# Value projection from the raw split of x, value weights ahead of token-major x, and an opening ordered by hand

## The chip, the cores and the metric

The kernel runs on one core of a Trainium2 chip. The metric is the device time of one execution in microseconds (us). "Before" is the kernel without the change, "after" the kernel with it. Both are written on top of a planner: the program states operations and tiles, and the planner assigns buffers, inserts the semaphores and orders the instructions of each engine by priority (program order) and by its own estimate of times, except inside blocks marked as a manual schedule, where the named engines keep the order of the program.

The five engines are TensorE (PE, with the weight loads as PEld), VectorE (DVE), ScalarE (ACT), GpSimd (POOL) and SyncE (SP), which issues nearly all DMAs.

## The reference

A trunk of two layers on one sequence of 512 tokens with 1024 channels, in float32. The change touches only the first step of the first layer, the forgetting attention:

```python
hn = rmsnorm(x, g[0])                      # x * rsqrt(mean(x*x) + 1e-6) * g
proj = hn @ w_in                           # w_in: 1024 x (3*1024 + 16): q, k, v, forget logits
f_logit = proj[..., 3*D:] + b_f            # 16 heads
log_f = log_sigmoid(f_logit)
c = cumsum(log_f, axis=1)
s = (q * 64**-0.5) @ k.T + c[:, None] - c[None, :]    # causal, per head of 64
o = softmax(s) @ v
...
x = x + rmsnorm(o @ w_out, g[1])
```

After it come a squared-ReLU MLP (1024 to 4096 to 1024) and a gated per-layer embedding, then a second layer of the same kind whose mixer is a gated short convolution.

## The kernel before

**Numbers as pairs.** A float32 operand of a matmul is split into a high part (rounded by ACT: a copy into the matmul's type) and a low part (the rest, a subtraction on DVE), and a product is three matmuls: high x high, high x low, low x high (`mm3`, `split`). For weights of the first projection the gain g of the norm is multiplied in while splitting (`split_gained`). x comes a second time from memory already transposed (`xT`, eight tiles of 128x512, `raw_x`), and its norm's factor 1/rms is applied later: to v when it leaves PSUM (`keep_values`), and to the transposed x itself (`normed_x`), which gives `hT`, the normalised and split x with tokens along the free dimension.

**Chunks of v.** v and the forget logits are computed for four blocks t of 128 tokens in three chunks of columns (`V_CHUNKS`): chunk 0 has 272 columns (256 of v and the 16 logits), chunk 1 has 512, chunk 2 has 256. Chunks 0 and 1 use the raw split `turned` (`of_x`) as the stationary operand, chunk 2 uses `hT`. Then `project(i)` makes q and k of heads 2i and 2i+1 from `hT`; `scores`, `turn` and `mix` are the attention itself. The split k (kh and kl) is copied by DMA to the other half of the partitions. `logs` computes log_f, `sums_of_logs` sums it by matmuls with a triangle of ones (`tri`), writes the sums to memory, and `bias(h)` reads them back as rows for head h.

**1/rms.** The mean squares come from x a third time, token-major (`first_x`, tiles xc): one half by ACT, one half by DVE (`mean_squares`), and the power -1/2 by POOL (`inverse`). `rows_of` makes a diagonal of them on POOL and a matmul with ones turns it into rows (bank `r_rows`) for `normed_x`.

**Loads and splits of weights.** `fetch(n)` issues the loads of weight tiles up to the n-th, in the order that `plan` recorded: chunk 0 of v (tiles 0 to 7), chunk 1 (8 to 15), chunk 2 (16 to 19, each two contraction tiles wide), then q and k (from 20 on, four tiles for each pair of heads), and so on. There are 14 buffers for raw weights, so tile n + 14 waits until tile n is split. `prepare(n)` splits up to the n-th.

**Order.** SP's queue begins with chunk 0's weights and xT, then four tiles of xc, then six of chunk 1's weights, then the other four of xc and the bias of the logits. A manual block holds PE, DVE, ACT and POOL in the program's order through chunk 0 up to the point where chunk 0's v is kept:

```python
        banks_v = [bank(f"v0_{t}") for t in range(NB)]
        with tc.manual_schedule(engines={E.PE, E.DVE, E.Activation, E.Pool}):
            ...
            for t in range(NB):
                keep_values(0, t, banks_v[t])
```

Behind that the planner orders: the triangle, the logs, chunk 1 with `rows_of` and `normed_x` between its blocks, the sums of logs, chunk 2, and `project(0)`. There are eight PSUM banks of 128x512 for everything and 70 SBUF pages of 128x512.

Of the kernel before, what the change touches and what calls it, by code (L numbers as in the profile page):

```python
# [8 lines left out]
F32 = mybir.dt.float32  # L9
# [6 lines left out]
P = 128  # L16
D = 1024
S = 512
# [50 lines left out]
def trunk(ctx: ExitStack, tc, x, xT, pT, g, gT, wv, wqk, bf, wo, wci, wcq, cw, wco, wup, wdn, wpp, wpg, out):  # L69
# [13 lines left out]
    def bank(name):  # L83
        return psum.tile([P, S], F32, tag="ps", name=name)
# [189 lines left out]
    def split(hi, lo, src, eng=nc.vector):  # L274

        nc.scalar.copy(hi, src)  # L276
        return eng.tensor_tensor(out=lo, in0=src, in1=hi.bitcast(F32), op=ALU.subtract)  # L277
# [131 lines left out]
                         f"{kind}r")  # L409
                then(t)  # L410

    def attention(hT, raw_x, first_x, b_f, work, by_hand):
        vs = [[None] * 4 for t in range(NB)]
        n_f = NB * H
        logit = stat("logit", n_f)
# [3 lines left out]
        def logs():  # L419

            e, u, lg = stat("f_e", n_f), stat("f_u", n_f), stat("f_l", n_f)
            neg = stat("f_n", n_f)
            nc.vector.tensor_scalar(out=neg, in0=logit, scalar1=-1.0, scalar2=None, op0=ALU.mult)
            nc.vector.tensor_tensor(out=neg, in0=logit, in1=neg, op=ALU.min)
            nc.scalar.activation(e, neg, AF.Exp)
            nc.vector.tensor_scalar(out=u, in0=e, scalar1=1.0, scalar2=None, op0=ALU.add)
# [5 lines left out]
            nc.vector.reciprocal(ru, u)  # L432
            nc.vector.tensor_tensor(out=rest, in0=rest, in1=ru, op=ALU.mult)
            nc.vector.tensor_tensor(out=lg, in0=lg, in1=rest, op=ALU.subtract)
# [4 lines left out]
            split(lf.hi, lf.lo, logf)  # L439

        def sums_of_logs(tri):
            ps_c = bank("ps_c")
# [23 lines left out]
        def of_x(k, t):  # L466
            return turned[t, k // 4].at(lambda h: h[:, k % 4 * P : k % 4 * P + P])

        def part(ps, t, n):

            for p, of in ("hi", "hi"), ("hi", "lo"), ("lo", "hi"):
                for k in range(4 * n, 4 * n + 4):
                    nc.tensor.matmul(
                        ps[:, : V_CHUNKS[0][1]], getattr(of_x(k, t), p),
                        getattr(ready["v", 0, k], of),
                        start=k == 0 and p == of, stop=k == KT - 1 and p == "lo",
                    )

        def values(c, t):

            width = V_CHUNKS[c][1]
            ps = bank(f"v{c}_{t}")
            for k in range(KT):
                if width == 256:
                    w = wide("v", c, k // 2).at(lambda u: u[:, k % 2 * 256 : k % 2 * 256 + 256])
                else:
                    w = wide("v", c, k)
                mm3(ps[:, :width], of_x(k, t) if c == 1 else tokens(hT, k, t), w, k == 0, k == KT - 1)
            keep_values(c, t, ps)

        def keep_values(c, t, ps):

            c0, width = V_CHUNKS[c]
            n_v = min(width, D - c0)
            if n_v < width:
                nc.vector.scalar_tensor_tensor(
                    out=logit[:, t * H : (t + 1) * H], in0=ps[:, n_v:width], scalar=rs[t],
                    in1=b_f, op0=ALU.mult, op1=ALU.add,
                )
            splits = []  # L500
            for c1 in range(0, n_v, 256):
                i = (c0 + c1) // 256
                vs[t][i] = page(f"v{t}_{i}", F32R)
                src = ps[:, c1 : c1 + 256].rearrange("p (i e d) -> p i e d", e=2, d=HD)
# [3 lines left out]
                    lo = block[:, :, 64 + 64 * e : 128 + 64 * e]  # L508
                    splits.append((hi, lo, src[:, :, e, :]))
            for hi, _, src in splits:  # L510
                if c < 2:
                    nc.scalar.mul(hi, src, rs[t])
                else:
                    nc.scalar.copy(hi, src)
            for hi, lo, src in splits:
                if c < 2:
                    nc.vector.scalar_tensor_tensor(
                        out=lo, in0=src, scalar=rs[t], in1=hi.bitcast(F32),
                        op0=ALU.mult, op1=ALU.subtract,
                    )  # L520
                else:
                    nc.vector.tensor_tensor(
                        out=lo, in0=src, in1=hi.bitcast(F32), op=ALU.subtract
                    )

        stacked, probs, outs, both = {}, {}, {}, {}

# [170 lines left out]
        name = "n0"  # L698
        E = mybir.EngineType

        def mean_squares(t):
            half = lambda n: first_x[t][n][:, :S]
            q = squares(half(0), f"{name}_q0_{t}"), products(half(1), f"{name}_q1_{t}")
            v = stat(f"{name}_v{t}")
            nc.vector.tensor_tensor(out=v, in0=q[0], in1=q[1], op=ALU.add)
            return v

        def inverse(t, v):
            r = stat(f"{name}_r{t}")
            nc.gpsimd.tensor_tensor(out=r, in0=v, in1=neg_half, op=ALU.pow)  # L710
            return r

        all_ones = page("all_ones")
        nc.gpsimd.memset(all_ones[:, :P], 1.0)
        r_rows = []

        def rows_of(t):
            if not r_rows:
                r_rows.append(bank("r_rows"))
            d = page(f"r_d{t}")  # L720
            nc.gpsimd.tensor_scalar(
                out=d[:, :P], in0=ident, scalar1=rs[t], scalar2=None, op0=ALU.mult
            )
            nc.tensor.matmul(
                r_rows[0][:, t * P : (t + 1) * P], all_ones[:, :P], d[:, :P],
                start=True, stop=True,
            )

        def normed_x(t):
            for n in range(2):  # L730
                h = raw_x[t][n][:, :S].rearrange("p (j c) -> p j c", j=4)
                r = r_rows[0][:, t * P : (t + 1) * P].unsqueeze(1).to_broadcast([P, 4, P])
                nc.vector.tensor_tensor(out=h, in0=h, in1=r, op=ALU.mult)
                to = lambda u: u[:, 4 * n : 4 * n + 4, t * P : (t + 1) * P]
                split(to(hT.hi), to(hT.lo), h)

        banks_v = [bank(f"v0_{t}") for t in range(NB)]
        with tc.manual_schedule(engines={E.PE, E.DVE, E.Activation, E.Pool}):
            work(9)
            split_x(0, 0)  # L740
            prepare(4)
            part(banks_v[0], 0, 0)
            split_x(0, 1)
            split_x(1, 0)
            part(banks_v[1], 1, 0)
            prepare(KT)
            part(banks_v[0], 0, 1)
            split_x(1, 1)
            part(banks_v[1], 1, 1)
            for t in (2, 3):  # L750
                for n in range(2):
                    split_x(t, n)
                    part(banks_v[t], t, n)
            for t in range(2):
                rs[t] = inverse(t, mean_squares(t))
                prepare(KT + 2 * t + 2)
            prepare(RAWS)
            for t in (2, 3):
                rs[t] = inverse(t, mean_squares(t))
            prepare(2 * KT)  # L760
            for t in range(NB):
                keep_values(0, t, banks_v[t])
        tri = page("tri", F32R)
        ones = page("ones")
        nc.gpsimd.memset(ones[:, :S], 1.0)
        nc.gpsimd.affine_select(
            out=ones[:, :S], in_=ones[:, :S], compare_op=ALU.is_ge, fill=0.0, base=0,
            pattern=[[1, S]], channel_multiplier=-1,
        )
        nc.vector.tensor_copy(tri[:, :S], ones[:, :S])  # L770
# [386 lines left out]
    with tc.manual_schedule(engines={mybir.EngineType.SP, mybir.EngineType.Activation}):  # L1157
# [13 lines left out]
        b_f = consts.tile([P, H], F32, tag="bf", name="b_f")  # L1171
        nc.sync.dma_start(b_f, bf[0:1, :].partition_broadcast(P))
    warm_p = bank("warm_p")

    def work(n):
# [6 lines left out]
    lhs, opened = attention(hT, raw_x, first_x, b_f, work, by_hand)  # L1182
    oT = lhs
    lhs = lambda k, t: tokens(oT, k, t)
    kind = "o"
# [120 lines left out]
```

## Time and profile before

| | us |
|---|---|
| median of 3 runs | 1230.01 |
| lowest and highest of them | 1228.50 and 1230.23 |
| the profiled execution | 1231.56 |
| its span, first to last instruction | 1229.8 |
| mean granted TensorE clock in it | 0.995 |
| PE busy from 0 to 100 us of the span | 91.38 |
| PE busy from 100 to 200 us | 100.00 |
| PE busy from 200 to 300 us | 98.75 |

The profile is of one execution. Times in its views count from the start of the span. A row of the timeline gives start, length, engine, line of the kernel, operation, written and read tiles, shapes, the number of instructions merged into the row, and in brackets how long the engine had been idle before and what ended that. Rows of SPq and ACTq are issues of DMAs. A row of the table of stretches gives the stretch, its length, busy time and number of instructions for each engine, the granted clock, the share of the DMA engines' time and their rate.

### The profile page before, as it was taken

The page shows a single profiled execution, that of the slowest core. Times are in us where ns is not written, and L with a number is a line of the kernel's source. Part 1 is how long each engine was busy: PE and PEld are TensorE (multiplying, and loading weights), DVE is VectorE, ACT ScalarE, POOL GpSimd, SP SyncE. Part 2 cuts the span into 40 slices and gives each one's busy share as a digit, 9 for nine tenths or more (in the row PEclk, how much of TensorE's full clock was granted, in tenths as well). Part 3 has the DMA queues.
Part 4 walks back from the last instruction along what each step waited for, and adds up shares of the span by engine and source line. Part 5 has one row for each costly group of instructions (what it writes and reads, how often), then busy time and mean ns, then how long its engine had stood idle before and what let it go on. Part 6 is the DMA issues. An engine that isn't in the chain of part 4 may idle for free.

```text
span 1229.8 us, 18755 instructions
## 1 busy us (share of the span) xinstructions
PE 1213.2 (99%) x6175; PEld 1030.7 (84%) x6175; DVE 932.0 (76%) x1474; ACT 690.2 (56%) x1465; POOL 657.1 (53%) x617
## 2 busy tenths in 40 slices
PE   8999999999999999999999999999999999999997
PEld 6778888798888888888889999989888888888886
DVE  6958889676787767869777798766876897669873
ACT  6747778656744644465567444445756345635551
POOL 2016566235876787866213255315677777778310
PEclk9899999999999999999999999999999999999999
DMA  9375554442343234328232133542422443245401
GB/s 313 122 184 152 153 170 130 145 164 70 120 138 95 82 99 137 120 65 288 76 104 88 50 102 96 155 159 91 129 75 71 138 137 95 61 120 164 179 8 61
DMA packets 87314, 150.84 MB, mean 123 GB/s; under 512 B 10352, under 2 KB 18080, under 8 KB 87216
## 3 DMA queue, kind: packets, MB, share of 16 engines
q1 hardware_dynamic: 86640, 149.11, 39.3%
q8 instruction: 49, 0.80, 0.3%
q10 hardware_dynamic: 576, 0.53, 0.1%
q14 instruction: 49, 0.40, 0.1%
HBM read 139.03 MB, written 6.37 MB: 118 GB/s over the span
## 4 chain that ended last, share of the span: by engine, by line
PE 88%; DMA 4%; issue 2%; DVE 2%; ACT 2%; POOL 2%; SPq 0%; POOLq 0%; DVEq 0%; ACTq 0%
PE up L268 9%; PE up L269 9%; PE up L270 9%; PE dn L268 8%; PE dn L269 8%; PE dn L270 8%; PE qk L270 2%; PE qk L269 2%; PE pg L268 2%; PE qk L268 2%; PE pg L270 2%; PE pg L269 2%; PE pT L597 1%; PE co L268 1%; PE co L269 1%
## 5 line engine op out<-in xcount | busy, mean ns | idle before, releaser
L277 DVE TENSOR_TENSOR wl<-raw,wh 128x512 fp32r<-128x512 f32 x346 | 347.5, 1049 | 14.2 <-ACT wh L276 13.4
L269 PE MATMUL up<-hTh,wl 128*128 128x512 f32 (+1 forms) x576 | 210.2, 365 | 0.0
L270 PE MATMUL up<-hTl,wh 128*128 128x512 f32 (+1 forms) x576 | 209.6, 365 | 0.0
L268 PE MATMUL up<-hTh,wh 128*128 128x512 f32 (+1 forms) x576 | 208.7, 366 | 0.0
L276 ACT CAST wh<-raw 128x512 fp32r<-128x512 f32 x346 | 189.4, 625 | 4.5 <-DVE xd L373 4.4
L958 ACT ACTIVATE r<-up 128x512 f32<-128x512 f32 (+1 forms) x72 | 39.4, 548 | 202.1 <-PE up L270 188.3
L277 POOL TENSOR_TENSOR wl<-dn_T,wh 128x512 fp32r<-128x512 f32 x96 | 132.7, 1414 | 30.1 <-ACT wh L276 30.1
L268 PEld LDWEIGHTS up<-hTh,wh 128*128 128x128 f32 x576 | 108.6, 189 | 17.6
L269 PEld LDWEIGHTS up<-hTh,wl 128*128 128x128 f32 x576 | 108.6, 189 | 17.4
L270 PEld LDWEIGHTS up<-hTl,wh 128*128 128x128 f32 x576 | 108.3, 189 | 17.6
L168 POOL TENSOR_TENSOR dn_T<-raw,raw 128x512 f32<-128x512 f32 x56 | 85.8, 1544 | 69.4 <-DMA raw<-in_wdn 58.1
L1004 DVE TENSOR_TENSOR acc<-dn,acc 128x512 f32<-128x512 f32 x168 | 107.4, 680 | 13.9 <-PE dn L270 13.8
L168 POOL TENSOR_TENSOR dn_T<-raw,dn_T 128x512 f32<-128x512 f32 x56 | 93.3, 1666 | 2.2
L276 ACT CAST wh<-dn_T 128x512 fp32r<-128x512 f32 x112 | 61.4, 616 | 11.0 <-POOL dn_T L168 11.0
L277 DVE TENSOR_TENSOR A12l<-q,A12h 128x512 fp32r<-128x512 f32 x28 | 22.3, 798 | 53.8 <-ACT A12h L276 53.8
L1018 POOL TENSOR_TENSOR acc<-acc,acc 128x512 f32<-128x512 f32 x28 | 46.9, 1709 | 9.9 <-DVE acc L1004 9.9
L270 PE MATMUL qk<-hTl,wh 128*128 128x512 f32 x128 | 51.1, 400 | 0.0
L269 PE MATMUL qk<-hTh,wl 128*128 128x512 f32 x128 | 51.1, 399 | 0.0
L268 PE MATMUL qk<-hTh,wh 128*128 128x512 f32 x128 | 50.7, 396 | 0.0
L269 PE MATMUL pg<-wh,hTl 128*128 128x512 f32 x128 | 50.5, 394 | 0.0
L268 PE MATMUL pg<-wh,hTh 128*128 128x512 f32 x128 | 50.4, 394 | 0.0
L277 DVE TENSOR_TENSOR A11l<-q,A11h 128x256 fp32r<-128x256 f32 x28 | 22.6, 807 | 36.5 <-ACT A11h L276 36.5
(413 smaller groups left out, 3328.7 us busy)
## 6 DMA issues: line engine op xcount, KB each, us to landing
raw<-in_wup SPq DMA_DIRECT2D x128, 256.0 KB, 2.9
raw<-in_wdn SPq DMA_DIRECT2D x128, 256.0 KB, 2.8
raw<-in_wcq SPq DMA_DIRECT2D x36, 256.0 KB, 2.8
raw<-in_wqk SPq DMA_DIRECT2D x32, 256.0 KB, 5.3
raw<-in_wpg SPq DMA_DIRECT2D x32, 256.0 KB, 4.4
g<-in_g SPq DMA_DIRECT2D x22, 256.0 KB, 5.7
prl<-neg_c SPq DMA_DIRECT2D x16, 256.0 KB, 6.4
raw<-in_wo SPq DMA_DIRECT2D x16, 256.0 KB, 3.9
```

Source lines behind the costliest of these rows:

```text
L168: ins = nc.gpsimd.tensor_tensor(out=B[name], in0=B[a], in1=B[b], op=op)
L268: nc.tensor.matmul(ps, a.hi, b.hi, start=start, stop=False)
L269: nc.tensor.matmul(ps, a.lo, b.hi, start=False, stop=False)
L270: nc.tensor.matmul(ps, a.hi, b.lo, start=False, stop=stop)
L276: nc.scalar.copy(hi, src)
L277: return eng.tensor_tensor(out=lo, in0=src, in1=hi.bitcast(F32), op=ALU.subtract)
L597: nc.tensor.transpose(ps[:, b * P : (b + 1) * P], probs[h][b][:, j * P : (j + 1) * P], ident)
L958: nc.scalar.activation(r[:, :n], ps[:, :n], AF.Relu)
L1004: ins = nc.vector.tensor_tensor(out=a, in0=banks[s], in1=a, op=ALU.add)
L1018: nc.gpsimd.tensor_tensor(out=a, in0=a, in1=acc[i, s][:, :S], op=ALU.add)
```

## The change

Chunk 2 of v is computed from the raw split too, and its 1/rms is applied when it leaves PSUM as for the other chunks, so `hT` is read only by `project`. The weights of v's second chunk are loaded ahead of all of xc, and those of the third behind it; SP is in the manual block as well. The block now reaches to the end of `normed_x` and to chunk 1's `keep_values`: its order for PE is chunk 0, chunk 1 (now by halves of the contraction, all products with the high weights first), with the matmuls for the rows of 1/rms once, in the middle of block 2. All mean squares are on ACT; `stats` does their end on POOL. The triangle is made at the start of POOL's work. The logs are cut into three steps between which chunk 1's blocks are kept. `normed_x` runs over one half of the channels for all four blocks, then the other. Outside the block stand chunk 2, with the sums of logs and the first two heads' bias after its second block, and `project(0)`.

```diff
-        def values(c, t):
-            width = V_CHUNKS[c][1]
-            ps = bank(f"v{c}_{t}")
+        def values(t):
+            ps = bank(f"v2_{t}")
             for k in range(KT):
...
-                mm3(ps[:, :width], of_x(k, t) if c == 1 else tokens(hT, k, t), w, k == 0, k == KT - 1)
-            keep_values(c, t, ps)
+                w = wide("v", 2, k // 2).at(lambda u: u[:, k % 2 * 256 : k % 2 * 256 + 256])
+                mm3(ps[:, :256], of_x(k, t), w, k == 0, k == KT - 1)
+            keep_values(2, t, ps)
...
-        def rows_of(t):
...
+        def inverse(t):
+            rs[t] = stats(t, first_x[t], name)
             nc.gpsimd.tensor_scalar(
+                out=r_d[:, t * P : (t + 1) * P], in0=ident, scalar1=rs[t], scalar2=None,
+                op0=ALU.mult,
             )
+        def rows():
+            ps = bank("r_rows")
+            for t in range(NB):
+                at = slice(t * P, (t + 1) * P)
+                nc.tensor.matmul(
+                    ps[:, at], warm[:, :P].bitcast(F32), r_d[:, at], start=True, stop=True
+                )
+            return ps
+        def normed_x(n, r_rows):
+            halves = [raw_x[t][n][:, :S].rearrange("p (j c) -> p j c", j=4) for t in range(NB)]
+            def low(t):
+                to = lambda u: u[:, 4 * n : 4 * n + 4, t * P : (t + 1) * P]
+                split(to(hT.hi), to(hT.lo), halves[t])
+            for t, h in enumerate(halves):
+                r = r_rows[:, t * P : (t + 1) * P].unsqueeze(1).to_broadcast([P, 4, P])
                 nc.vector.tensor_tensor(out=h, in0=h, in1=r, op=ALU.mult)
+                if t:
+                    low(t - 1)
+            low(NB - 1)
...
+        with tc.manual_schedule(engines={E.PE, E.DVE, E.Activation, E.Pool, E.SP}):
...
             prepare(KT)
-            part(banks_v[0], 0, 1)
+            fetch(2 * KT)
+            first_x = [load_x("xc", t) for t in range(NB)]
+            nc.sync.dma_start(b_f, bf[0:1, :].partition_broadcast(P))
+            fetch(2 * KT + 4)
+            halves(0, (0, 1))
...
+            nc.vector.tensor_copy(tri[:, :S], ones[:, :S])
+            prepare(KT + 4)
+            halves(1, (0, 0), (1, 0))
             prepare(2 * KT)
+            halves(1, (0, 1), (1, 1))
             for t in range(NB):
-                keep_values(0, t, banks_v[t])
...
-        logs()
+                inverse(t)
+            halves(1, (2, 0))
+            r_rows = rows()
+            halves(1, (2, 1), (3, 0), (3, 1))
+            for two in ((0, 1), (2, 3)):
+                for t in two:
+                    logits(t, banks_v[0, t])
+                for t in two:
+                    keep_values(0, t, banks_v[0, t])
+                prepare(2 * KT + 4)
+            steps = logs()
+            next(steps)
+            keep_values(1, 0, banks_v[1, 0])
+            next(steps)
+            keep_values(1, 1, banks_v[1, 1])
+            next(steps)
+            normed_x(0, r_rows)
+            keep_values(1, 2, banks_v[1, 2])
+            normed_x(1, r_rows)
+            keep_values(1, 3, banks_v[1, 3])
         for t in range(NB):
-            values(1, t)
-            if t in (0, 2):
-                rows_of(t)
-                rows_of(t + 1)
-            if t:
-                normed_x(t - 1)
-        sums_of_logs(tri)
-        normed_x(3)
-        bias(0)
-        bias(1)
-        for t in range(NB):
-            values(2, t)
+            values(t)
+            if t == 1:
+                sums_of_logs(tri)
+                bias(0)
+                bias(1)
         for _ in project(0):
             pass
...
             if t == 1:
                 fetch(KT)
-        first_x = [load_x("xc", t) for t in range(2)]
         fetch(RAWS)
-        first_x += [load_x("xc", t) for t in (2, 3)]
```

More of the change, by code (lines that the diff above doesn't have):

```diff
@@ L699, in attention @@
         E = mybir.EngineType
[L701 to L711, printed above, removed]
@@ L713, in attention @@
-        all_ones = page("all_ones")
-        nc.gpsimd.memset(all_ones[:, :P], 1.0)
-        r_rows = []
-        def rows_of(t):
-            if not r_rows:
-                r_rows.append(bank("r_rows"))
-            d = page(f"r_d{t}")
+        r_d = page("r_d")
+        def inverse(t):
+            rs[t] = stats(t, first_x[t], name)
             nc.gpsimd.tensor_scalar(
-                out=d[:, :P], in0=ident, scalar1=rs[t], scalar2=None, op0=ALU.mult
-            )
[L724 to L727, printed above, removed]
@@ L735, in normed_x, with halves @@
-                split(to(hT.hi), to(hT.lo), h)
-        banks_v = [bank(f"v0_{t}") for t in range(NB)]
-        with tc.manual_schedule(engines={E.PE, E.DVE, E.Activation, E.Pool}):
+                if t:
+                    low(t - 1)
+            low(NB - 1)
+        with tc.manual_schedule(engines={E.PE, E.DVE, E.Activation, E.Pool, E.SP}):
             work(9)
+            banks_v = {(0, t): bank(f"v0_{t}") for t in range(NB)}
+            def halves(c, *at):
+                for t, n in at:
+                    if (c, t) not in banks_v:
+                        banks_v[c, t] = bank(f"v{c}_{t}")
+                    part(c, banks_v[c, t], t, n)
@@ L748, in attention @@
             split_x(1, 1)
-            part(banks_v[1], 1, 1)
+            halves(0, (1, 1))
             for t in (2, 3):
@@ L752, in attention @@
                     split_x(t, n)
[L753 to L759, printed above, removed]
+                    halves(0, (t, n))
+            tri, ones = page("tri", F32R), page("ones")
+            nc.gpsimd.memset(ones[:, :S], 1.0)
+            nc.gpsimd.affine_select(
+                out=ones[:, :S], in_=ones[:, :S], compare_op=ALU.is_ge, fill=0.0, base=0,
+                pattern=[[1, S]], channel_multiplier=-1,
+            )
```

69 lines of the change are left out of this document (23 added, 46 removed).

## The prediction

> **What bounds the kernel now.** I read the page first, then a table of stretches, then the waits and the timelines of the first 90 us, engine by engine. The page's first part says who is the bound:
>
> ```profile
> PE 1213.2 (99%) x6175; PEld 1030.7 (84%) x6175; DVE 932.0 (76%) x1474; ACT 690.2 (56%) x1465; POOL 657.1 (53%) x617
> ```
>
> TensorE has work in all but 16.6 of 1229.8 us, so a change elsewhere counts only where TensorE stands still or runs slow. The change touches the opening alone. The stretches there are v's first chunk, its second chunk, its third chunk with the sums of logs, then q and k of the first heads, then the first scores. Columns: stretch and its length; busy time with instructions of PE, PEld, DVE, ACT, POOL; granted clock; DMA share; GB/s.
>
> ```profile
> 0.00:19.40 19.40, 17.52 (x106) 15.32 (x107) 10.69 (x21) 11.49 (x21) 1.44 (x9) 1.00 0.89 300
> 19.40:45.80 26.40, 24.14 (x105) 18.09 (x104) 22.09 (x62) 19.23 (x51) 6.38 (x9) 1.00 0.84 281
> 45.80:65.40 19.60, 17.39 (x112) 15.80 (x111) 17.21 (x44) 10.70 (x30) 0.29 (x1) 0.83 0.16 20
> 65.40:81.00 15.60, 15.57 (x70) 12.55 (x68) 8.57 (x19) 9.29 (x22) 2.47 (x7) 1.00 0.78 228
> 81.00:87.80 6.80, 4.58 (x15) 3.81 (x16) 3.50 (x12) 3.54 (x7) 0.70 (x2) 0.75 0.63 158
> ```
>
> The third and fifth stretch also lose clock. Busy time overstates TensorE, since the ends are modelled, so I count spacings from its timeline (start, length, engine, line, operation, tiles, shapes, count, idle before).
>
> ```profile
> 19.39 0.40 PE L268 MATMUL v<-wh,xh 128*128 128x512 f32 x1
> ...
> 26.30 0.50 PE L268 MATMUL v<-wh,xh 128*128 128x512 f32 x1 [1.74 <-ACT wh L285]
> ...
> 36.03 0.39 PE L268 MATMUL v<-wh,xh 128*128 128x512 f32 x1
> ...
> 38.08 0.39 PE L268 MATMUL v<-wh,xh 128*128 128x512 f32 x1
> ...
> 45.78 0.40 PE L445 MATMUL ps_c<-tri,lf_h 128*16 128x512 f32 x1
> ...
> 47.17 0.33 PE L268 MATMUL v<-wh,hTh 128*128 128x256 f32 x1
> ...
> 47.93 0.28 PE L268 MATMUL v<-wh,hTh 128*128 128x256 f32 x1
> ...
> 50.09 0.30 PE L268 MATMUL v<-wh,hTh 128*128 128x256 f32 x1
> 51.21 0.38 PE L268 MATMUL v<-wh,hTh 128*128 128x256 f32 x1 [0.81 <-ACT hTh L276]
> ...
> 54.57 0.58 PE L269 MATMUL v<-wh,hTl 128*128 128x256 f32 x1 [0.60 <-DVE hTl L277]
> ...
> 65.37 0.40 PE L270 MATMUL qk<-hTl,wh 128*128 128x512 f32 x1
> ...
> 82.23 0.30 PE L581 MATMUL sc<-kh,qs 128*128 128x128 f32 x1 [1.26 <-DMA kh<-kh]
> 83.52 0.33 PE L582 MATMUL sc<-kl,qs 128*128 128x128 f32 x1 [1.00 <-DMA kl<-kl]
> ```
>
> Nine matmuls of 512 columns lie between 36.03 and 38.08: 0.228 us each. Eighteen of 256 columns lie between 47.93 and 50.09: 0.120 each. The second chunk has 4 blocks x 8 tiles x 3 products = 96 matmuls of 512 columns, 21.9 us; it took 45.78 - 19.39 = 26.4. The matmuls for the rows of 1/rms in it are worth some 0.7, so 3.8 us are lost, 1.74 of them at one stop for a late weight. From 47.17 to 65.37 the third chunk took 18.2 us for 96 matmuls of 256 columns (11.5) and four qk ones set between them (0.9): 5.8 lost, about 3 in stops for the normalised x (hT) and the rest at a halved clock. **Together 9.6 us** between 19.4 and 65.4 are no work. A third loss comes at the first scores: 1.26 + 1.00 of idle and, at clock 0.75, 0.25 x 6.8 = 1.7 of slow matmuls, together 4.0.
>
> **The change part by part.**
>
> *Loads.* v's second-chunk weights move ahead of the token-major x. On the queue of SP and on ACT and DVE the order was:
>
> ```profile
> 8.76 2.14 SPq L381 DMA_DIRECT2D xc<-in_x  x4
> ...
> 16.85 2.81 SPq L381 DMA_DIRECT2D xc<-in_x  x4
> ...
> 14.18 1.28 ACT L276 CAST xh<-xT 128x512 fp32r<-128x512 f32 x2 [1.84 <-DMA xT<-in_xT]
> ...
> 18.19 1.37 ACT L285 ACTIVATE wh<-raw,first_g 128x512 fp32r<-128x512 f32 x2 [1.97 <-DMA raw<-in_wv]
> ...
> 19.46 0.62 ACT L312 ACTIVATE junk<-xc 128x512 f32<-128x512 f32 x1
> 19.98 0.18 ACT L312 ACTIVATION_READ_ACCUMULATOR junk<-xc 128x1 f32 x1
> ...
> 25.53 1.38 ACT L285 ACTIVATE wh<-raw,first_g 128x512 fp32r<-128x512 f32 x2 [1.32 <-DMA raw<-in_wv]
> ...
> 18.95 1.42 DVE L287 SCALAR_TENSOR_TENSOR wl<-raw,first_g,wh 128x512 fp32r<-128x512 f32 x2 [1.79 <-ACT wh L285]
> ```
>
> Five transfers of 256 KB (four of xc and the first weight) lie between xT's last landing at about 14.5 and 18.15: 0.735 each. Without the four, weights 8 to 15 land from 15.2 to 20.4, the eight of xc by 26.3, b_f at 26.4, the third chunk's four weights by 29.3. On SP weights 14 and 15 wait for the buffers of weights 0 and 1, whose splits stand ahead of nearly all of x: no stop. ACT is free of x at 15.5 and splits a weight in 0.65 to 0.69, DVE in 0.7: weights 8 to 11 are done at about 19.3, with TensorE at 19.39; 12 to 15 at about 22.1, needed at 19.39 + 24 x 0.228 = 24.9. The 3.8 us go. What is late next is xc: ACT's eight squares (0.62 and a read of 0.18, overlapping by some 0.1) follow the landings, from 22.5 for block 0 to 27.0 for block 3. POOL then has three steps a block, two on 128x1 and the diagonal, of which the last is:
>
> ```profile
> 27.50 2.81 POOL L721 TENSOR_SCALAR r_d<-ident,n_r 128x128 f32<-128x128 f32 x4
> ```
>
> At 0.7 for each of the twelve they end by 22.5 + 8.4 = 30.9. The rows' matmuls come at 24.9 + 5.5 + 2.7 = 33.1, so TensorE's own work hides them with 2 us to spare. With four banks for chunk one, three for chunk two and one for the rows, block 3 of chunk two needs a bank that `keep_values(0, 0)` frees; DVE can start on that when b_f is in at 26.5 and ends at about 28.1, while TensorE wants it at 33.1 + 0.6 + 2.7 = 36.4. Nothing is lost there, and it would take 8 us more to lose anything. Moving the tri mask to the start of POOL's queue costs DVE a copy of 0.4 behind which weight 8 waits; that is within the cover above to some 0.1 us. So the second chunk ends at 19.39 + 21.9 + 0.6 = 41.9 instead of 45.8.
>
> *Third chunk from the raw split.* It no longer reads hT, so it follows at once: 11.5 us, and the sums of logs 1.4 (45.78 to 47.17). TensorE reaches q and k at 54.8. The 5.8 us go, and the price is that DVE must have hT and the first wqk tile by then. In DVE's queue, by these rows:
>
> ```profile
> 34.32 0.55 DVE L432 RECIPROCAL f_ru<-f_u 128x64 f32<-128x64 f32 x1
> ...
> 42.50 1.13 DVE L517 SCALAR_TENSOR_TENSOR v<-v,n_r,v 128x128 fp32r<-128x128 f32 x4 [0.32 <-ACT v L512]
> ...
> 48.63 3.67 DVE L733 TENSOR_TENSOR xT<-xT,r_rows 128x512 f32<-128x512 f32 x6
> ...
> 53.25 0.67 DVE L450 COPY c_T<-ps_c 16x512 f32<-16x512 f32 x1
> 53.85 3.68 DVE L277 TENSOR_TENSOR hTl<-xT,hTh 128x512 fp32r<-128x512 f32 x6
> ...
> 58.64 3.24 DVE L287 SCALAR_TENSOR_TENSOR wl<-raw,first_g,wh 128x256 fp32r<-128x256 f32 x8
> ```
>
> from 26.5 on stand, in the order written: chunk one kept (8 x 0.28 and four logits, 3.1), four weight tiles (8 x 0.41 = 3.3), the logs (nine steps on 128x64, of which this is the longest: under 5, I take 2.1), chunk two kept (16 x 0.28 = 4.5), hT (8 x 0.61 twice, 9.8). That is 22.8 us of work. It waits besides for ACT's halves, for the third chunk's weights until 29.3, for ACT's table load ahead of Ln, and for block 3 of chunk two at 41.9; following these steps in order I get hT whole at about 53 and the list's end at 54.8. Tile by tile q and k want hT's second half only at 54.8 + 12 x 0.228 = 57.5: covered by 4. The first wqk tile, behind the list, is split at 55.6: TensorE waits 0.8 for it. Bounds: 0, if the planner sets that tile into one of DVE's waits, and 1.3 of wait with clock loss behind it. I take 0.6, near the walk. Later tiles cost DVE 0.82 and TensorE 1.37, so it doesn't fall behind again.
>
> What a wait costs in clock is where row and rule differ. At 54 to 56 us the clock is down after stops of 0.8 at most:
>
> ```profile
> 54.00:56.00 2.00, 1.43 (x6) 0.50 0.00 0
> ```
>
> By the 1.7 us of slow matmuls behind the scores' stops, 1.3 of wait could cost 3.0. The Trainium skill ("TensorE: Matmul & The Clock Gate", Part 1: The HAM clock gate) has the clock halve after an idle window of about 3.4 us; by that the wait of 0.8 costs itself alone and the sum stays what it is. The trace disagrees in part: no single stop here was that long, several short ones in a row were enough.
>
> *Rest of the diff.* Squares on ACT instead of half on DVE, and the scale by 1/rms in keeping chunk three (16 instructions, each no dearer than chunk two's 0.28): below 1 us on engines with cover. DVE's four products and sums of them that go free nothing that anyone waits for.
>
> *First scores.* They come 72 qk matmuls behind 54.8, at 71.2; now it is 65.37 + 68 x 0.228 = 80.9. They wait for kh and kl copied across partitions:
>
> ```profile
> 65.96 7.90 SPq L158 DMA_DIRECT2D raw<-in_wqk  x7
> 74.52 0.53 SPq L553 DMA_DIRECT2D kh<-kh  x1
> ...
> 71.25 0.68 DVE L277 TENSOR_TENSOR kl<-qk,kh 64x512 fp32r<-64x512 f32 x1 [1.48 <-ACT kh L276]
> ```
>
> kl was ready at 71.9, its copy queued behind seven weights on SP. k of the first heads ends on TensorE as far ahead of the scores as before, SP still refills the weight buffers in between, and DVE is busier (about 8 wqk tiles at 0.82 and chunk three behind the list). So the loss of 4.0 can go (copies issued at once) or grow by some 3 to 6 (DVE's backlog). I take it as unchanged.
>
> **Sum:** 9.6 - 0.6 = 9.0 us off. The profiled run took 1231.56 (span 1229.8 and 1.76 around it), so 1222.6; it lies 1.55 above the median of the runs, 1230.01, so for the median **1221.0**. Its own range: 13.6 off if the scores' stop goes too (1216.4), 6 off if the wait costs 3.0 and clock (1224).
>
> **The rivals.** *DVE becomes the bound.* It was busy 17.2 of 19.6 us in the third stretch; the same work, less 8 us of time. For it: the walk ends 0.8 late already. Against: 65.4 to 81.0 shows 8.6 of 15.6 busy, room to catch up. If kl is made 4 to 6 us later against TensorE than before, the gain is 9.0 less that: 3 to 5 off, 1225 to 1227.
>
> *The bias of the logs comes too late (slower).* From the start of c_T (53.25) to the last mask of head 0 took 16.3 us:
>
> ```profile
> 69.01 0.49 POOL L569 TENSOR_SCALAR_AFFINE_SELECT prl<-prl 128x128 f32<-128x128 f32 x1 [0.73 <-DMA prl<-neg_c]
> ```
>
> That used to be ready 12.7 us before the first scores (82.2). Now TensorE is 9.6 earlier, and c_T stands on DVE behind the list and perhaps behind eight wqk tiles: 54.8 + 6.6 = 61.4, ready at 77.7. Without bias DVE can't empty the scores' banks; TensorE goes on through six banks of about 1.7 us (six qk matmuls and two scores), to 81.4. From c_T at 65.1 on each us costs one; at 74.1 the gain is gone, at 79 it is 5 slower: 1235. Against it: 13 us of delay on DVE that I see no work for.
>
> *The loads don't bring it.* If the weights landed no earlier, 3.8 of the 9.6 stay: 5.2 off, 1224.8. Against: the spacing of 0.735 leaves room on each tile. I count it with the first rival.
>
> **How the numbers follow.** About 0.2% (2.5 us) is what a measurement of this kernel can tell from no change. Forecast 0.63; DVE as the bound or late loads, still over 2.5 faster, 0.19; most of the gain lost, within 2.5, 0.05; the late bias or another loss of that sign in the newly ordered rest 0.13. The range goes from 1217.0 (13 off) to 1228.0, which takes in the forecast's range and the first rival and leaves the last two cases out.
>
> **What would show it.** Right: no stop of TensorE above 0.5 us from 19.4 to 54, the last v matmul near 54 and the 72nd qk one near 71, clock 1.00 in 50 to 60, ACT's first 512-wide weight near 16, xc issued behind all of wv1. Wrong: a stop for hT or wl of over 2 us at the first qk matmul, scores waiting beyond 77, a mask on neg_c as the releaser of DVE's score steps, or a part behind 100 us that became longer.

## The result: the opening came forward as predicted, the time did not

| | before | after |
|---|---|---|
| median, us | 1229.96 | 1231.87 |
| lowest and highest | 1227.55 and 1232.10 | 1229.94 and 1233.45 |
| runs | 13 | 13 |
| span of the profiled execution | 1229.8 | 1230.4 |
| mean granted clock in it | 0.995 | 0.994 |

The ratio of after to before is 1.0018, with an interval of 1.0009 to 1.0026: slower by 0.1 to 0.3%. The forecast was 1221.0, its range 1217.0 to 1228.0. The result lies outside.

The table of stretches of after, cut at the points that answer to those of before (columns as there):

```profile
0.00:20.42 20.42, 18.74 (x105) 16.96 (x106) 14.65 (x26) 15.57 (x27) 1.81 (x9) 1.00 0.93 306
20.42:43.12 22.70, 22.70 (x106) 18.91 (x105) 13.04 (x43) 15.89 (x46) 6.31 (x12) 1.00 0.74 263
43.12:55.84 12.72, 12.72 (x105) 12.22 (x104) 11.76 (x26) 9.02 (x23) 0.00 (x0) 1.00 0.01 3
55.84:72.35 16.51, 16.51 (x74) 13.34 (x72) 13.87 (x36) 12.52 (x33) 0.88 (x3) 1.00 0.59 173
72.35:83.38 11.03, 0.00 (x0) 0.03 (x1) 0.00 (x0) 1.01 (x1) 1.47 (x5) 0.64 0.75 192
83.38:90.20 6.82, 6.16 (x19) 5.07 (x20) 5.03 (x17) 3.78 (x11) 1.55 (x2) 0.58 0.40 108
```

Rows two to four are the change at work: from 20.42 to 72.35 TensorE has no gap and the full clock. Before, q and k of the first heads ended at about 81.0 (65.37 and 68 matmuls of 0.23); after, they end at 72.35, 8.6 us earlier. Row five is where it goes: 11.03 us in which TensorE does nothing, VectorE too. Row six is the slow clock behind that.

TensorE's waits in the first 100 us of after (engine, written tile, line, what released it: us in total, times, longest):

```profile
PE sc L574 <- DMA kh<-kh: 11.0, 1, 11.0
PE warm_p L1182 <- DVE warm L1164: 1.5, 1, 1.5
PE sc L575 <- DMA kl<-kl: 0.7, 1, 0.7
PE v L476 <- ACT wh L285: 0.2, 1, 0.2
```

All stops that the change aimed at are gone. What is left is the wait of the first scores for the copies of kh and kl, 2.26 us before and 11.7 now. The copies land at nearly the same time in both kernels: the first score step starts at 82.23 before and at 83.38 after. From there on the two run alike: the first product with v is at 100.0 and 101.5, the first matmul of `up` at 263.8 and 264.4. A gain of 8.6 us in TensorE's arrival has become a wait.

SP's queue in after, and ScalarE's cast of kh, show why the copies don't come earlier:

```profile
61.87 1.73 SPq L461 DMA_DIRECT2D neg_c<-neg_c  x4
65.00 0.34 SPq L561 DMA_DIRECT2D prr<-neg_c  x1
...
68.99 0.78 SPq L561 DMA_DIRECT2D prl<-neg_c  x1
69.87 5.69 SPq L158 DMA_DIRECT2D raw<-in_wqk  x3
75.65 0.53 SPq L546 DMA_DIRECT2D kh<-kh  x1
76.27 0.64 SPq L158 DMA_DIRECT2D raw<-in_wqk  x1
77.00 0.70 SPq L546 DMA_DIRECT2D kl<-kl  x1
```
```profile
64.01 0.61 ACT L276 CAST kh<-qk 64x512 fp32r<-64x512 f32 x1
```

kh is cast by 64.6, but its copy is issued at 75.65. Ahead of it stand the stores of `neg_c`, the eight loads of `bias(0)` and `bias(1)` from 65.00 to 69.77, and weights, whose three issues now take 5.69 us (an issue at 66 in before took 0.82). Then the copy itself takes long. In the part on DMA issues (KB each, median us from issue to landing), for 60 to 86 us of after:

```profile
prl<-neg_c SPq DMA_DIRECT2D x2, 256.0 KB, 8.5
kh<-kh SPq DMA_DIRECT2D x2, 128.0 KB, 7.0
kl<-kl SPq DMA_DIRECT2D x2, 128.0 KB, 6.5
```

From 69 to 77.9 us SP waited for 0.2 us in all: what held the first head's kh and kl were the issues ahead of them, which took that long. SP's waits of over half a microsecond from 69 to 80 us name the bias loads, but they belong to the copies of the second head, issued at 78.39 and 79.58:

```profile
SPq L546 <- DMA prl<-neg_c: 0.7, 1, 0.7
SPq L546 <- DMA prr<-neg_c: 0.6, 1, 0.6
```

The copies need nothing of the bias. In the program's list of waits the completion semaphores of the DMAs are handed out in turn, eight of them, and a DMA waits until the one eight issues ahead of it has landed. The times agree: eight issues ahead of these two copies stand the bias loads of 68.52 and 68.99, which landed 9.8 and 10.5 us later, at 78.3 and 79.5. That is how a copy comes to wait for a bias load; no run here takes this sharing away by itself.

### The profile page after: what moved, and what is told of

Same layout as the page of the kernel before. It is cut to its first block, busy times and chain, and to the rows that moved or that the text cites. A ratio compares the mean times of both kernels' runs of the same rounds, so it can differ in the third digit from the quotient of the medians.

```text
span 1230.4 us, 18747 instructions
## 1 busy us (share of the span) xinstructions
PE 1209.3 (98%) x6175; PEld 1030.8 (84%) x6175; DVE 928.4 (75%) x1462; ACT 694.1 (56%) x1473; POOL 657.7 (53%) x620
## 4 chain that ended last, share of the span: by engine, by line
PE 88%; DVE 3%; issue 3%; ACT 2%; POOL 2%; DMA 1%; SPq 0%; POOLq 0%; ACTq 0%; DVEq 0%
PE up L270 9%; PE up L268 9%; PE up L269 9%; PE dn L268 8%; PE dn L270 8%; PE dn L269 8%; PE v L476 2%; PE qk L269 2%; PE qk L270 2%; PE qk L268 2%; PE pg L269 2%; PE pg L268 2%; PE pg L270 2%; PE pT L590 1%; PE co L270 1%
## 5 line engine op out<-in xcount | busy, mean ns | idle before, releaser
L277 DVE TENSOR_TENSOR wl<-raw,wh 128x512 fp32r<-128x512 f32 x346 | 345.2, 1043 | 14.6 <-ACT wh L276 13.9
L276 ACT CAST wh<-dn_T 128x512 fp32r<-128x512 f32 x112 | 61.4, 616 | 10.9 <-POOL dn_T L168 10.9
```

## The experiments

Each run is compared with runs of the kernel before on the same chip. **Theory Q**: the bias loads, which wait for `c_T` and `neg_c`, stand ahead of the copies, delay their issue and slow their landing; so the copies land near 83 whenever TensorE arrives. **Rivals**: the copies are late because `c_T` is late on VectorE; because of the queue on which they are issued; because of the weights ahead of them; or the new order has cost something elsewhere.

| kernel | first kh issued | first score | stop there | first ps_o | first `up` | median | ratio to before, interval |
|---|---|---|---|---|---|---|---|
| before | 74.5 | 82.2 | 1.3 + 1.0 | 100.0 | 263.8 | | |
| after | 75.7 | 83.4 | 11.0 + 0.7 | 101.5 | 264.4 | 1231.87 | 1.0018, 1.0009 to 1.0026 |
| e1_bias_behind | 64.0 | 71.1 | none | 89.9 | 255.3 | 1223.76 | 0.9952, 0.9937 to 0.9967 |
| e2_one_behind | 70.8 | 78.3 | 7.1 + 0.8 | 96.1 | 260.5 | 1228.39 | 0.9994, 0.9985 to 1.0003 |
| e3_copies_act | 72.7 | 81.1 | 9.5 + 1.1 | 99.6 | 263.3 | 1230.13 | 1.0007, 0.9998 to 1.0017 |
| e4_sums_early | 74.9 | 83.0 | 9.7 | 101.5 | 265.1 | 1230.97 | 1.0009, 0.9999 to 1.0018 |
| e5_bias_in_block | 67.2 | 73.8 | 1.5 + 0.8 | 92.7 | 256.1 | 1222.64 | 0.9944, 0.9926 to 0.9962 |
| e6_before_bias_behind | 67.4 | 76.8 | none | 91.8 | 255.3 | 1224.43 | 0.9962, 0.9947 to 0.9977 |
| e7_before_weights_first | 74.6 | 81.6 | 2.5 + 0.8 | 100.2 | 263.6 | 1231.55 | 1.0015, 1.0005 to 1.0025 |
| e8_block_soon4 | 65.1 | 72.7 | none | 89.0 | 252.3 | 1220.19 | 0.9922, 0.9907 to 0.9936 |
| e9_soon4 | 69.4 | 78.5 | 7.5 | 99.3 | 262.0 | 1230.39 | 1.0009, 0.9999 to 1.0018 |
| e10_behind_soon4 | 63.6 | 71.1 | none | 91.6 | 256.3 | 1224.56 | 0.9961, 0.9947 to 0.9975 |
| e11_before_behind_soon4 | 69.7 | 79.1 | none | 98.1 | 262.6 | 1229.47 | 0.9996, 0.9986 to 1.0005 |

"First score" is the first matmul of the first head's scores, "first ps_o" the first product with v, `up` the first matmul of the MLP; these columns, in us, are of one profiled execution each. "None" means under 0.2 us.

**Taking the bias loads out of the way.** e1 puts both heads' loads behind `project(0)`, e2 only the second's:

```diff
             if t == 1:
                 sums_of_logs(tri)
-                bias(0)
-                bias(1)
         for _ in project(0):
             pass
+        bias(0)
+        bias(1)
```

> After, with the eight bias loads of heads 0 and 1 issued behind project(0), so that the copies of kh and kl stand ahead of them on SP. Theory Q (the copies are late because they stand on SP behind the bias loads, which themselves wait for c_T at 59.6): kh is issued near 66 instead of 75.7, TensorE's stop at the first score falls from 11.0 to 1 to 4 us, and the time falls by 5 to 9 us, to 1223 to 1227. Rival W (the weights of q and k fill the DMA engines and the copies land late wherever they stand): kh still lands near 83, the stop stays above 8 us, the time stays within 2 us of after. Rival B (the bias is what is next): kh lands early, but DVE's first score steps wait for the bias until about 85 and TensorE stops there for 6 us or more.

> After, with the four bias loads of head 1 alone moved behind project(0); head 0's four stay ahead of the copies. Theory Q: half of the way between after and the run with all eight behind: kh issued near 70 to 72, TensorE's stop 5 to 8 us, time 2 to 5 us below after. Rival W: as after, stop 11 us. Rival B: no different from all eight behind.

e1 brings the time down to 1223.76. kh is issued at 64.01, 0.5 us after its cast ends, and the copies land faster. Its DMA part for 60 to 84 us:

```profile
kh<-kh SPq DMA_DIRECT2D x4, 128.0 KB, 3.4
kl<-kl SPq DMA_DIRECT2D x3, 128.0 KB, 3.6
```

The first score follows the last qk matmul at 71.1 without a stop. e2 lies between: four loads ahead of the copies instead of eight, kh issued 4.8 earlier than in after, the stop 7.1. So the bias loads are a cause, and by their number.

**Another queue, an earlier c_T.** e3 lets ScalarE issue the four copies of `project(0)`; e4 moves `sums_of_logs` into the hand-ordered block, the loads directly behind the block:

```diff
-                            nc.sync.dma_start(h[b, :S].bitcast(F32), h[a, :S].bitcast(F32))
+                            (nc.scalar if i == 0 else nc.sync).dma_start(
+                                h[b, :S].bitcast(F32), h[a, :S].bitcast(F32)
+                            )
```
```diff
             normed_x(0, r_rows)
             keep_values(1, 2, banks_v[1, 2])
+            sums_of_logs(tri)
             normed_x(1, r_rows)
```

> After, with the copies of kh and kl of the first two heads issued by ACT's queue instead of SP's; in the program's semaphores the kh copy still waits for the landing of the bias load four issues earlier (the completion semaphores of DMAs are taken in turn, eight of them). Theory Q in its simple form (position on SP's queue is what delays the copy): kh is issued at 65, stop of TensorE under 3 us, time 7 to 10 us below after. Theory Q in the other form (the semaphore taken in turn, so the copy waits for a bias load to land, whichever queue issues it): kh is issued at 73 to 75 as before, ACT stands still for that long, stop 9 to 11 us, time within 2 us of after or slower. Rival W: as the second.

> After, with the sums of logs (their matmuls behind chunk 1, c_T and neg_c on DVE between the two halves of hT) inside the manual block, so that c_T stands at about 46 instead of 59.6 us, and the bias loads directly behind the block. Theory Q: neg_c is stored by 50 and the bias loads run by 62, the copies find SP free at 66 to 68, TensorE's stop falls to 1 to 4 us; hT and the first weight tile come 2 us later and cost TensorE at most 1; time 6 to 9 us below after, 1223 to 1226. Rival W: stop stays above 8 us. Rival B: as Q, since the bias is early here too.

e3 gains little: ScalarE has cast kh at 65.5 and issues its copy at 72.68. The chain that ended last in e3 (start, us, what), from 67 us:

```profile
67.00 8.76 DMA pr<-neg_c
75.83 6.83 DMA kl<-kl
```

Eight issues ahead of kh in the program stands the first head's `prl`, ahead of kl the second head's `pr`, which is the one in the chain. The issues of `prl`, kh and kl, and the time from issue to landing of that `prl`:

```profile
66.10 0.37 SPq L563 DMA_DIRECT2D prl<-neg_c  x1
72.68 0.52 ACTq L546 DMA_DIRECT2D kh<-kh  x1
75.83 0.47 ACTq L546 DMA_DIRECT2D kl<-kl  x1
```
```profile
prl<-neg_c SPq DMA_DIRECT2D x1, 256.0 KB, 6.5
```

So `prl` lands at 72.6 and `pr` at 75.76, and each copy goes out within 0.1 us of that, though kh was cast by 65.5 and kl made by 68.5. The order of the one queue was not all that held the copies; the shared semaphores account for both times here, eight issues back and not four as the expectation has it. e4 missed its expectation. `neg_c` was stored at 48 instead of 62, but the loads were issued only from 61.8 on, behind weights that waited for their splits, so still ahead of the copies, and the stop was 9.7. Not the time of c_T decides, but where the loads stand.

**Both: loads early in the block.** e5 adds `bias(0)` and `bias(1)` to e4's block, directly behind the sums. e6 and e7 are made from the kernel before: e6 with only the bias loads behind `project(0)`, e7 with only the change's order of loads (those six of v's second-chunk weights that find a free buffer ahead of all xc):

```diff
             keep_values(1, 2, banks_v[1, 2])
+            sums_of_logs(tri)
+            bias(0)
+            bias(1)
             normed_x(1, r_rows)
```
```diff
-        first_x = [load_x("xc", t) for t in range(2)]
         fetch(RAWS)
-        first_x += [load_x("xc", t) for t in (2, 3)]
+        first_x = [load_x("xc", t) for t in range(4)]
```

> After, with the sums of logs and also the eight bias loads of heads 0 and 1 inside the manual block, between the two halves of hT, so that SP issues the bias loads right behind neg_c, near 50 us, where the DMA engines stand idle, and nothing of them lies ahead of the copies of kh. Theory Q (the copies are late because of the bias loads ahead of them, not because of when c_T is made): kh is issued near 66 to 68 behind three weight loads that wait for splits, lands by 72 to 75, TensorE's stop is 1 to 3 us, and since the bias is early too, the stop of 2.2 us at the first mix that the run with the bias behind had (at 89) goes as well: 9 to 11 us below after, 1220 to 1223. Rival W (weights on the DMA engines delay the copies wherever they stand): kh lands near 80 or later, stop above 6 us, no more than 4 us below after.

> Before, with the eight bias loads moved behind project(0), and nothing else. Theory Q: the 2.3 us of idle and the slow clock at before's first scores have the same cause; kh is issued near 71 instead of 74.5, the stop goes, and the time falls by 2 to 4 us below before; a later stop, since the bias now comes late, may take 1 or 2 of that back. Rival W: the copies land as late as before, no change.

> Before, with only the loads exchanged: chunk 1's weights ahead of all of the token-major x. Its own 3.8 us upstream: TensorE's stops between 19.4 and 45.8 us go, by at least 2 us. Theory Q (what is gained ahead of the scores is given back where the copies wait): the copies are tied to the bias loads and through them to c_T on DVE, which moves less than TensorE does; the stop at the first scores grows by 1 to 3 us and the time falls by 0 to 2 us only. Rival (the gains upstream simply carry through): 3 to 4 us below before.

e5 issues the loads from 49.3 to 54.3, and the time is 1222.64. A stop of 1.5 and 0.8 is left: eleven weights now stand ahead of kh. e6 is the sharpest result: without any of the change, moving two lines gives 1224.43, and TensorE starts the scores at 76.8 without a stop. That is 5.2 us below before, more than the 2 to 4 expected, and kh is issued at 67.41 and not near 71. Of the 5.4 us by which the scores start earlier, 1.3 are the stop for kh; 4.2 came ahead of that, in the third chunk, where the clock now stayed at 1.00 with stops of 0.21 and 0.85 instead of 0.81, 0.81 and 0.60. Part of the 9.6 us that the prediction counted thus hung on the clock, which stayed up here with 1.2 us less of stops. Why moving the bias loads shortened the stops at hT is not shown; the planner orders that part. e7 did not do upstream what was expected of it. The stops in the second chunk did not go: those above 0.2 us add up to 3.4, against 2.2 in before, and most now wait for VectorE's half of the split, the longest ahead of 28.03:

```profile
28.03 0.50 PE L270 MATMUL v<-wl,xh 128*128 128x512 f32 x1 [1.69 <-DVE wl L287]
```

Behind them the matmuls run at half speed from 30.0 to 33.5, and the chunk ends at 48.55 instead of 45.78. The third chunk keeps its clock, so TensorE still reaches the scores at 79.1, 1.8 us earlier than in before; there it stops for 3.3 us instead of 2.3, and the clock from 81 to 88 is 0.52 instead of 0.76. The first score is at 81.6 and the time is within 0.3% of before, on the slow side. This order of loads alone brings nothing, but as a test of theory Q it had only 1.8 us to give back.

**The weights ahead of the copies.** Four copies and weights share the queue in `project(0)`, which asks for raw weights eight tiles ahead. e8 (on top of e5) and e9 (on top of after) ask for four:

```diff
-                        ps, narrow("qk", i, k=k, c=s * P),
+                        ps, narrow("qk", i, k=k, c=s * P, soon=SOON if i else 4),
```

> The block with the sums and the bias loads in it, as in e5_bias_in_block, and project(0) asks for raw weights only four tiles ahead, so that the four copies of the first head's q and k stand ahead of the raw loads of tiles 42 to 45 on the queue. If the copies are late because of what stands ahead of them on the queue (theory Q), kh is issued at 64 to 66 and kl at 65 to 68, the first score step starts without a stop near 71.5, the clock after it stays above 0.9, and the time is 2 to 4 us below e5_bias_in_block: 1218 to 1221. If the rest is set by the making of kl on VectorE behind the tile splits (rival), kl is made at 67 as before, a stop of about 0.8 and the slow clock stay, and the time is 1222 to 1223.

> The changed kernel, project(0) asks for raw weights only four tiles ahead, so that the copies stand ahead of the last raw loads; the bias loads stay ahead of the copies. Theory Q (the bias loads, which wait for neg_c, hold the copies): kh is issued at 70 to 73, the stop at the first score is still 6 to 9 us, the clock falls to 0.5 after it, and the time is 0 to 3 us below the changed kernel's: 1229 to 1232. Rival W (the raw loads of the weights hold them): kh is issued by 67, the stop falls below 3 us, and the time is 5 or more below: 1222 to 1227.

Both came out as theory Q had it, e8's first score 1 us later and e9's kh 0.6 earlier than expected. In e9 kh is issued directly behind the last bias load, with no weight between, and still TensorE stops:

```profile
69.43 0.91 SPq L546 DMA_DIRECT2D kh<-kh  x1
70.43 2.88 SPq L546 DMA_DIRECT2D kl<-kl  x1
...
78.52 0.45 PE L574 MATMUL sc<-kh,qs 128*128 128x128 f32 x1 [7.47 <-DMA kh<-kh]
```

The first score starts 9.1 us after kh's issue, behind bias loads of 1.28 MB (twice 64, 128, 192 and 256 KB), and the time stays at before's. So the weights alone were not what held them. In e8, with the bias loads early and the weights behind, kh is issued at 65.10 and kl at 65.82, and the first score comes right behind the last qk matmul:

```profile
72.46 0.39 PE L270 MATMUL qk<-hTl,wh 128*128 128x512 f32 x1
72.69 0.22 PE L574 MATMUL sc<-kh,qs 128*128 128x128 f32 x1
```

No stretch of 5 us from 60 to 100 has a clock below 1.00 there. e8 is the fastest kernel of this study, 1220.19: 0.6 to 0.9% below before, and below after.

**What the change is worth with the copies free.** e10 is e1 and e11 is e6, both with the weights four tiles ahead, so that two more kernels differ by the change alone.

> The changed kernel with the bias loads behind project(0), as in e1_bias_behind, and raw weights asked for only four tiles ahead in project(0). The copies have the queue to themselves already in e1_bias_behind, so by theory Q the first score step stays at 71 to 72 without a stop. If the stop of 2.2 us at the first product with v and the slow clock behind it were a matter of the queue, they go and the time is 1219 to 1221; if they come from the planner's order of ScalarE and VectorE, the time stays at 1222 to 1225.

> The kernel before, with the same two edits (bias loads behind project(0), raw weights only four tiles ahead). Here the first score step had no stop at 76.8 in e6_before_bias_behind. Theory: with the copies out of the way on both sides, the change is worth what is left of v's stops, 4 to 5 us; this kernel takes 1223.5 to 1226. Rival: the full 9.6 us of the prediction's opening come back (stops at hT and half clock as in the kernel before); then it takes 1228 to 1231.

e10 came out as its second case: the stop at the first product with v stays, and the second pair of heads has a new one for its kh, which is issued behind eight weights at 80.60. These are the two rows of its waits:

```profile
PE sc L574 <- DMA kh<-kh: 2.5, 1, 2.5
PE ps_o L613 <- ACT ph L594: 2.1, 1, 2.1
```

The chain of e10 leads to the second from the last bias load, issued at 70.46 and landed 9.43 us later, through masks and scaling on GpSimd to the rounding `ph` on ScalarE. Bias loads that come too late for the softmax are the other side of the same choice; with e8's early loads 1.1 us of this stop is left. e11 missed its expectation, 1223.5 to 1226, by 3.5 and fell into its rival's range: its slow clock in the third chunk came back in part (0.73 in 54 to 60, after stops of 0.81 and 0.85), and it got the same 2.2 us stop at the first product with v, which e6 does not have. So pairs that differ by the change alone give three answers: after against before 1.9 slower, e1 against e6 0.7 faster at the medians of two chips, with overlapping intervals, e10 against e11 4.9 faster with intervals apart. The change has no one price; it has one for each order of the queue behind it. Why e11 has the late rounding and e6 has not, though both have the bias loads in the same place, stays open. So does what the kernel before would gain from bias loads as early as e8's, which was not tried.

## Why the prediction was wrong

**Loads and second chunk: right, 1 us late.** The chunk was predicted from 19.39 to 41.9, 22.5 us; it ran from 20.42 to 43.12, 22.7. The rows' matmuls came at 34.06, against 33.1. The 1.0 at the start arises in chunk 0, where sixteen matmuls from 7.5 us on ran at 0.227 spacing; the prediction did not look there.

```profile
7.53 1.11 PE L476 MATMUL v<-wl,xh 128*128 128x272 f32 x4
...
34.06 1.05 PE L707 MATMUL r_rows<-r_d,warm 128*128 128x128 f32 x8
...
55.84 0.63 PE L268 MATMUL qk<-hTh,wh 128*128 128x512 f32 x2
```

**Third chunk and the price on VectorE: right, a little dear.** 12.72 us with the sums of logs, against 11.5 and 1.4. q and k were predicted at 54.8 and began at 55.84, with no stop: hT was whole at 52.2 (predicted 53), the list ended at 53.6 (54.8), so the 0.6 us for the first wqk tile did not fall due. VectorE's queue:

```profile
50.75 1.46 DVE L277 TENSOR_TENSOR hTl<-xT,hTh 128x512 fp32r<-128x512 f32 x2
52.56 1.13 DVE L514 SCALAR_TENSOR_TENSOR v<-v,n_r_y,v 128x128 fp32r<-128x128 f32 x4 [0.35 <-ACT v L512]
53.61 6.03 DVE L287 SCALAR_TENSOR_TENSOR wl<-raw,first_g,wh 128x256 fp32r<-128x256 f32 x15
59.55 0.67 DVE L453 COPY c_T<-ps_c 16x512 f32<-16x512 f32 x1
```

**First scores: here it failed.** The step "I take it as unchanged" held the loss of 4.0 fixed while TensorE came 9 earlier. It was the term of the sum that was mis-sized: the stops became 11.03 and 0.66 instead of 1.26 and 1.00, and the clock behind them was 0.58 instead of 0.75. Counted as the prediction counts them, that is 11.03 + 0.66 + 0.42 x 6.82 = 14.6 us instead of 4.0. The 10.6 more outweigh the 8.6 that TensorE had won, by 2.0; the medians differ by 1.9. The argument was that k ends on TensorE as far ahead of the scores as before. That is true and did not matter, since the copies were not waiting for k. The chain of before, which the prediction did not quote, says so:

```profile
66.88 10.21 DMA raw<-in_wqk
77.15 6.33 DMA kl<-kl
```

The path to the first score runs back through a weight load and not through a qk matmul. Kl was ready at 71.9 and issued at 77.15. The 71.9, the 74.52 of kh's issue and the seven weights between stood in the prediction; they were the sign that the copies belong to the queue's time and not to TensorE's. Nor did the queue stay where it was: c_T, 53.9 before, was done at 60.2, and SP issued the eight bias loads from 65.00 on instead of from 59.59. In before they were through by 65.86, ahead of kh's cast; in after they stand between the cast and the copy. The bound given, "grow by some 3 to 6 (DVE's backlog)", was too small and named the wrong cause: kl was made at 67.6 in after and issued at 77.0.

**The late bias: right chain, wrong victim.** c_T was done at 60.2, against 61.4 predicted. The rival let the bias block VectorE and the score banks, from a delay of c_T to 65 on. Nobody waited for the masks in after; VectorE waited for TensorE's scores (14.1 us, `prr` on `sc`). The bias loads hurt through what stands behind them on SP. Their cost in this order is e1's difference to after, 8.1 us at the median. DVE as the bound and late loads did not occur. The 0.13 for "the late bias or another loss of that sign" is the case that came, by a path that was not worked out. One slip has no bearing on this: "6 off" reads as 9.0 less 3.0, but 0.6 of that wait is already out of the 9.0; from 9.6 it is 6.6 off.

**What was said to show it.** No stop from 19.4 to 54 above 0.5 us, the 72nd qk matmul near 71 (72.0), clock 1.00: all right. "Scores waiting beyond 77": that one, listed under wrong, came.

## What to carry to other kernels

A stage that comes forward gains only if all that its next stage waits for comes forward too: for each operand of that next stage, follow the chain back to what sets its time, and if it ends in a queue that the change does not bring forward, take the arrival as fixed, or later if the change moves loads into its way, and the wait as growing. On a queue shared by urgent small copies and large loads, place the copies ahead of what is needed later, and look what the loads moved behind them will then be late for. And try the cheap edit on the old kernel too: e6 shows that much of such a gain may not need the change.

## What the hardware showed that was not expected

**Loads that have not landed slow what is issued behind them.** The same 128 KB copy landed 3.4 us after issue in e1 and 7.0 behind the eight bias loads in after. The first kh of e9, directly behind the bias loads, and of e5, behind eleven weights:

```profile
kh<-kh SPq DMA_DIRECT2D x1, 128.0 KB, 9.0
```
```profile
kh<-kh SPq DMA_DIRECT2D x1, 128.0 KB, 6.5
```

So it is not the bias loads alone: in e5 the last of them had landed 4 us before kh's issue. They are slow by themselves, though. That last one was issued at 53.54 and landed 9.7 us later; from 54 to 56.5 us, before the first weight is issued, the DMA engines' share was 0.74 at 130 GB/s, and with the weights, from 63 to 66, it was 1.05 at 396. An issue itself also stretched: 2.88 us for kl in e9, 3.08 for a weight in after, 0.46 to 0.53 for the copies in e8, with nothing in the profile's list for it to wait for. Whether the number of transfers under way or their small packets limit this was not tried.

**The clock falls after short stops, but not after each.** After 11 us of stop in after the clock was down 3 to 4 us into it, and stayed at half until 88:

```profile
72.00:76.00 4.00, 0.35 (x2) 0.00 (x0) 0.00 (x0) 1.35 (x2) 0.88 (x3) 0.93 0.63 168
76.00:80.00 4.00, 0.00 (x0) 0.00 (x0) 0.00 (x0) 0.00 (x0) 0.59 (x2) 0.50 0.90 241
80.00:84.00 4.00, 0.45 (x1) 0.29 (x1) 0.00 (x0) 0.00 (x0) 0.00 (x0) 0.50 0.66 159
84.00:88.00 4.00, 3.51 (x10) 3.10 (x11) 2.88 (x11) 2.54 (x8) 0.62 (x1) 0.50 0.19 49
```

That agrees with the idle window of about 3.4 us that the Trainium skill gives ("TensorE: Matmul & The Clock Gate", Part 1: The HAM clock gate). In e5 stops of 1.5 and 0.8 us sufficed (0.57 from 74 to 82), in e8 one of 1.1 did not (1.00 throughout), and of two stops of similar length the longer cost no clock, 1.74 us in before, and the shorter did, 1.5 in e6. The rows are those for 20 to 30 us, first of before, then of e6:

```profile
20.00:30.00 10.00, 7.74 (x30) 4.67 (x29) 8.03 (x20) 6.29 (x16) 6.08 (x9) 1.00 0.97 328
```
```profile
20.00:30.00 10.00, 8.20 (x29) 5.69 (x28) 7.43 (x20) 6.12 (x15) 6.48 (x9) 0.83 1.04 362
```

By that rule of the Trainium skill a stop has to fill a window of about 3.4 us; the trace disagrees there, since 1.5 us was enough in e6. The same section of the Trainium skill calls the window free-running, so that it does not start anew with the kernel. Whether that decides which of two short stops costs clock, no run here shows. For a forecast it means that a stop of 1 to 3 us has two prices, with and without slow matmuls behind it: 0.83 over the 10 us of e6 is 3.4 us at half clock.
